# Moving mLSTM's row operations behind the GLA scores in a hybrid decoder step

## The chip, the cores and the metric
The kernel runs on one core of one Trainium2 chip. Its time is the device time of one execution in microseconds, the median of several runs. Five engines work beside each other, each from a queue of its own that it takes in order: TensorE (PE; PEld is its weight load), VectorE (DVE), ScalarE (ACT), GpSimd (POOL) and SyncE (SP, which here only issues transfers).

## The reference
One step of a decoder trunk with two layers, for 512 prompt tokens and 8 sequences of 4 sample tokens, 544 columns in all. Layer 0 ("ab") mixes tokens with two groups of heads, mLSTM and GLA (gated linear attention), layer 1 with a Mamba-2 mixer; each is followed by an MLP. The change is in layer 0's mixer:

```python
mq, mk, mv, mo, mi, mf, gq, gk, gv, gg, ga = split(x @ w_in)      # one projection
# mLSTM, 4 heads of 64 x 128
ig = mi + ig_bias;  lf = log_sigmoid(mf + fg_bias)
b = cumsum(lf);  D = b[t] - b[s] + ig[s]  (s <= t);  m = max(b + m0, max_s D)
s = (q @ k.T) * exp(D - m);  h = (s @ v + ...) / max(|den|, exp(-m))
C = exp(...) * C0 + sum_s exp(D[last, s] - m[last]) * k[s] v[s]
# GLA, 4 heads of 64 x 128
la = log_sigmoid(ga @ wa2 + ba) / 16;  A = cumsum(la)             # per key channel
s[t, s] = sum_k q[t, k] k[s, k] exp(A[t, k] - A[s, k])  (s <= t)
o = s @ v + (q * exp(A)) @ S0
```

## The kernel before
**Dense work.** Activations lie feature-major: 128 features on the partitions, 544 tokens in two halves of 272 (`hf` 0 and 1). A dense product in full precision is three matmuls per 128-deep step: each operand is split into a high part (`whi`, `xh`) and a remainder (`wlo`, `xl`). The projection of layer 0 has 24 weight tiles; each takes 2 halves x 24 matmuls. A tile is loaded by SP (`wraw`), cast by ScalarE (`whi`, L167), and its remainder is taken by VectorE (`wlo`, L168); five tiles are kept ready. The products leave PSUM by ScalarE (L817, L828).

**Lanes.** Everything else in the layer is written as generators, the lanes, which run between the dense matmuls. Before each dense matmul `tick()` moves every lane by one; a lane that yields W["x"] continues W["x"] + 1 matmuls later, and `need(key)` holds it until another lane has marked the key ready. So the order of TensorE's work is counted in dense matmuls by the table `W`. The other engines' order is made by the framework's planner from its own cost model: the earliest ready instruction first, in the order of the program; `tc.high_priority()` moves instructions ahead, and `hold("head")` (L1129, `tc.issue_after`) queues what stands in it behind the last head's last instruction on the same engine.

**The gates.** `gate_sums` (L837) forms the gate columns of the projection for each half, and `gate_rows` (L848) spreads them to rows by one matmul (L852) and copies them with bias into `gate` (L853). When both halves are there, the GLA lane and the mLSTM lane start.

**The GLA lane.** `gla_decay` (L1028) multiplies the gate by wa2 (`la`, L1036), takes the logarithm of the sigmoid and a scan along the tokens (`A`, L1042). `gla_scores` (L1046) works through two halves of the heads, q = 0 and 1. For each it forms the diagonal products (`gd`, L1073), then nine levels of block sizes 1, 2, 4 to 256. For a level GpSimd subtracts (`F`, L1084), ScalarE takes two exponentials (L1086, L1087), VectorE makes the two operands (`zq` L1091, `zk` L1093), and W["lev"] matmuls later TensorE multiplies them (`gs`, L1101, for the last level L1114); the result goes into the score tile `sT` (L1105 and others). W["s0"] is the distance from the start to the first diagonal products. At the end of each half the key ("gT", q) is marked, and behind the second "gscores".

**The heads.** `head_out` (L857) multiplies scores and values (`num`, L868), takes statistics on VectorE (`bst`, `bmv`, `hb`) and normalises on ScalarE (`hf` L878, `hn` L896); 49 matmuls later the result is transposed (`hot`, L902). GLA's heads 0 and 1 follow ("gT", 0), heads 2 and 3 follow ("gT", 1); a head's emission marks ("g", h).

**The mLSTM lane.** `ml_gates` (L1216) works on rows: four partitions (one for each head) of 544 tokens, in the tiles `rw` and `uw`. Block one takes the logarithm of the sigmoid (L1225 to L1228), the scan b (L1229), u = ig - b (L1230) and a running maximum by a second scan (L1236). Block two forms m (L1240), stores it (p_m L1241, s_m L1244), and forms exp(-m) (L1246) and the state weights (L1249 to L1253). Block three (L1257 to L1271) prepares the transposes and the sample tokens. W["gates"] + 1 matmuls after head 3, `uw` is transposed (`uwt`, L1279) to columns for the mLSTM heads, which run after GLA's. In block one the lane waits for ("g", 0), in block two for ("g", 1), in block three for ("g", 2).

## Time and profile before

| | |
|---|---|
| median of 3 runs | 1496.58 us (1495.94 to 1497.34) |
| profiled execution | 1497.35 us, its span 1495.6 us |
| mean granted TensorE clock | 0.994 |
| TensorE busy | 1465.4 us, 98% of the span |
| VectorE, ScalarE, GpSimd busy | 1100.7, 793.6, 190.4 us |
| TensorE's waits in the first 130 us | level products for zk 9.0 us in 2 waits, the longest 7.4; the first matmul 1.1; xh 0.6; la 0.6; gates 0.3 |

Layer 0's mixer fills about the first 260 us. A row of the timeline reads: start, duration, engine, line, operation, what it writes and reads, number of instructions, and in brackets how long the engine stood idle before it and what released it. In a row of waits stand the total, the number and the longest. A row of stretches has the stretch, its length, then for each engine its busy time with the number of instructions, and at the end the granted TensorE clock, the share of the transfer engines and GB/s.

### The profile page before, as it was taken

To read this page: it belongs to the slowest core of one execution; us is meant where nothing else is said; L and a number is where in the kernel's file an instruction comes from. 1 tells how busy PE (TensorE), PEld (TensorE's weight loads), DVE (VectorE), ACT (ScalarE), POOL (GpSimd) and SP (SyncE) were. 2 spreads that over 40 slices of the span, in tenths; PEclk is the share of its full clock that TensorE was granted. 3 is DMA by queue.
4 is the path that set the end of the run, shared out by engine and by line. 5 is a ranking of instruction groups with operands and counts; after the bars stand their busy time and mean duration, and the time that the engine had idled before them with its cause. 6 is when DMAs were issued, how large, how long until landed. Compare 5 with 4: busy or idle time off the path is not lost.

```text
span 1495.6 us, 29198 instructions
## 1 busy us (share of the span) xinstructions
PE 1465.4 (98%) x11607; PEld 1416.8 (95%) x11607; DVE 1100.7 (74%) x2075; ACT 793.6 (53%) x1750; POOL 190.4 (13%) x228
## 2 busy tenths in 40 slices
PE   9989999999999999999999999999999999999997
PEld 8979999999999999999888789899999999999996
DVE  6675676787677667678899978777688677676656
ACT  7455366483444544547786676555257354444343
POOL 2320132100000000010233341421010000000000
PEclk9989999999999999999999999999999999999998
DMA  7202333313233322425557766364222233233121
GB/s 241 81 32 75 100 117 106 104 50 103 87 101 95 100 86 85 156 67 188 130 172 230 246 179 227 99 214 143 71 76 71 96 100 99 85 100 98 59 86 60
DMA packets 95025, 172.51 MB, mean 115 GB/s; under 512 B 15880, under 2 KB 50968, under 8 KB 94632
## 3 DMA queue, kind: packets, MB, share of 16 engines
q1 hardware_dynamic: 62280, 140.44, 29.9%
q10 hardware_dynamic: 29216, 17.19, 4.4%
q0 software_dynamic: 3392, 13.00, 2.4%
q8 instruction: 91, 1.49, 0.4%
q14 instruction: 46, 0.38, 0.1%
HBM read 153.48 MB, written 17.13 MB: 114 GB/s over the span
## 4 chain that ended last, share of the span: by engine, by line
PE 42%; DVE 5%; DMA 2%; issue 1%; ACT 1%; POOL 0%; ACTq 0%; SPq 0%; DVEq 0%; POOLq 0%
PE psd L378 29%; PE psd L590 9%; DMA E<-d_cs 1%; PE yp L1710 1%; PE it L1757 1%; DVE wlo L168 1%; DVE acc L1604 1%; DMA ec<-d_ecs 1%; PE sp L1688 1%; PE sps L1764 1%; DVE h0n L1770 0%; PE ip L1685 0%; ACT E L1670 0%; DVE xf L552 0%; PE xt L1649 0%
## 5 line engine op out<-in xcount | busy, mean ns | idle before, releaser
L378 PE MATMUL psd<-xh,whi 128*128 128x272 f32 x1488 | 440.5, 296 | 0.6 <-ACT xh L287 0.6
L378 PE MATMUL psd<-xl,whi 128*128 128x272 f32 x1488 | 433.8, 292 | 1.3 <-DVE xl L478 1.3
L378 PE MATMUL psd<-xh,wlo 128*128 128x272 f32 x1488 | 434.5, 292 | 0.0
L378 PEld LDWEIGHTS psd<-xh,whi 128*128 128x128 f32 x1488 | 280.5, 189 | 8.4 <-issue 5.1
L378 PEld LDWEIGHTS psd<-xl,whi 128*128 128x128 f32 x1488 | 280.8, 189 | 7.7 <-issue 4.2
L378 PE MATMUL psd<-hh,whi 128*128 128x272 f32 x992 | 286.6, 289 | 0.0
L378 PE MATMUL psd<-hlo,whi 128*128 128x272 f32 x992 | 286.1, 288 | 0.0
L378 PE MATMUL psd<-hh,wlo 128*128 128x272 f32 x992 | 286.0, 288 | 0.0
L378 PEld LDWEIGHTS psd<-xh,wlo 128*128 128x128 f32 x1488 | 280.6, 189 | 4.1 <-issue 3.2
L168 DVE TENSOR_TENSOR wlo<-wraw,whi 128x1024 fp32r<-128x1024 f32 (+2 forms) x175 | 207.3, 1187 | 58.4 <-ACT whi L167 57.4
L167 ACT CAST whi<-wraw 128x1024 fp32r<-128x1024 f32 (+2 forms) x175 | 173.5, 997 | 129.8 <-PE psd L378 115.2
L378 PEld LDWEIGHTS psd<-hh,whi 128*128 128x128 f32 x992 | 186.8, 188 | 0.2
L378 PEld LDWEIGHTS psd<-hlo,whi 128*128 128x128 f32 x992 | 186.7, 188 | 0.2
L378 PEld LDWEIGHTS psd<-hh,wlo 128*128 128x128 f32 x992 | 186.7, 188 | 0.1
L428 DVE TENSOR_TENSOR xf<-xf,psd 128x272 f32<-128x272 f32 x208 | 88.2, 434 | 74.2 <-PE psd L378 73.6
L590 PE MATMUL psd<-xh,wlo 128*128 128x272 f32 x416 | 119.9, 288 | 0.0
L590 PE MATMUL psd<-xh,whi 128*128 128x272 f32 x416 | 119.8, 288 | 0.0
L590 PE MATMUL psd<-xl,whi 128*128 128x272 f32 x416 | 119.6, 288 | 0.0
L203 ACT CAST whi<-wsum 128x1024 fp32r<-128x1024 f32 x52 | 54.3, 1044 | 110.8 <-PE psd L590 70.1
L203 ACT CAST whi<-wraw 128x1024 fp32r<-128x1024 f32 (+1 forms) x52 | 43.4, 834 | 95.3 <-PE psd L378 84.2
L204 DVE TENSOR_TENSOR wlo<-wsum,whi 128x1024 fp32r<-128x1024 f32 x52 | 63.7, 1225 | 23.2 <-ACT whi L203 23.2
L590 PEld LDWEIGHTS psd<-xl,whi 128*128 128x128 f32 x416 | 78.4, 188 | 0.0
(488 smaller groups left out, 2829.7 us busy)
## 6 DMA issues: line engine op xcount, KB each, us to landing
wraw<-mlp_w SPq DMA_DIRECT2D x80, 512.0 KB, 3.6
wraw<-ssd_in SPq DMA_DIRECT2D x40, 512.0 KB, 4.3
wraw<-mlp_w SPq DMA_DIRECT2D x64, 256.0 KB, 2.9
wraw<-ab_in SPq DMA_DIRECT2D x22, 512.0 KB, 3.8
h<-h SPq DMA_DIRECT2D x32, 256.0 KB, 4.2
h0n<-h0n SPq DMA_DIRECT2D x16, 512.0 KB, 4.3
E<-d_cs ACTq DMA_DIRECT2D x16, 512.0 KB, 5.2
s_h<-h0n POOLq DMA_DIRECT2D x16, 512.0 KB, 4.5
```

The source lines that it names most:

```text
L167: nc.scalar.copy(hi[:, r], w[:, r])
L168: nc.vector.tensor_tensor(lo[:, r], w[:, r], hi[:, r].bitcast(F32), ALU.subtract)
L203: self.cut[0] = nc.scalar.copy(hi, x).ins
L204: self.cut[1] = nc.vector.tensor_tensor(lo, x, hi.bitcast(F32), ALU.subtract).ins
L378: last[0] = TE.matmul(ps[:, :TH], (hi, hi, lo)[t][:, k, :], (rh, rl, rh)[t], start=i == 0, stop=i == n - 1).ins
L428: V.tensor_tensor(x, x, ps, ALU.add)
L590: last[0] = TE.matmul(ps, wt[:, k], bt[:, k], start=first and n == 0, stop=n == 11, skip_group_check=not first).ins
L1604: V.scalar_tensor_tensor(acc[:, :n], ci[:, w:w + n], cw[:, m, w:w + 1], acc[:, :n], ALU.mult, ALU.add)
L1688: TE.matmul(sp, Bt[:, b], xw, start=True, stop=True)
L1710: TE.matmul(ypv[64 * e:64 * e + 64, j], z[:, 64 * r:64 * r + 64], E[:, r], start=True, stop=True)
L1757: TE.matmul(it[64 + NS * k:64 + NS * k + NS], Cm[:, NS * (q + k):NS * (q + k) + NS], h0[k], start=q == 0, stop=q == NB - 2)
L1764: TE.matmul(sp[:, 256 * j:256 * j + 256], Xs[:, m * P:(m + 1) * P], Bm.rearrange("p k n -> p (k n)"), start=True, stop=True)
```

## The change
The gates' first half is spread between the first tile's and the second tile's second half, the second half in the middle of the third tile; before, both came behind the second tile. Their two copies get high priority. Block one of the row operations waits for "gscores" and block two for ("g", 2), so that all three blocks are issued behind head 2. W["s0"] goes from 50 to 42, W["lev"] from 15 to 16.

```diff
-W = dict(... lev=15, ... s0=50, ...)
+W = dict(... lev=16, ... s0=42, ...)
@@ gate_rows
-            S.activation(gate[:, c0:c1], p[:, :TH], AF.Identity, bias=gbias)
+            with tc.high_priority():
+                S.activation(gate[:, c0:c1], p[:, :TH], AF.Identity, bias=gbias)
@@ ml_gates
             S.copy(u, gate[0:4])
-            yield from need(("g", 0))
+            yield from need("gscores")
             with hold("head"):
...
-            yield from need(("g", 1))
+            yield from need(("g", 2))
             with hold("head"):
                 m = b
@@ the layer's loop
                 if (hf, m) == (1, 0):
                     for _ in gate_sums(1):
                         pass
-        for hf in range(2):
-            gate_rows(hf)
+                    gate_rows(0)
         for m, key in enumerate(order[:-4]):
             if m >= HEADA:
                 w = ws.next()
                 for hf in range(2):
                     dense(w, xrhs, KT, hf, lambda h, p, m=m: evac(m, h, p))
+                    if (m, hf) == (HEADA, 0):
+                        gate_rows(1)
```

## The prediction
> **What bounds the kernel now.** I read the first part of the page, then the strip of 40 slices, then TensorE's waits, and last the timeline around the one wait that is large.

> ```profile
> span 1495.6 us, 29198 instructions
> PE 1465.4 (98%) x11607; PEld 1416.8 (95%) x11607; DVE 1100.7 (74%) x2075; ACT 793.6 (53%) x1750; POOL 190.4 (13%) x228
> PE gs L1101 <- DVE zk L1093: 9.0, 2, 7.4
> PE la L1036 <- ACT gate L853: 0.6, 1, 0.6
> PE gates L852 <- ACT gsum L846: 0.3, 1, 0.3
> ```

> TensorE is busy 98% of the span, so a change that removes no matmul can only win back idle time or lost clock: 1495.6 - 1465.4 = 30 us are idle in all. In the rows of TensorE's waits, the part that this change touches has three: level products (gs) waiting for VectorE's zk, twice, and two short ones at the gates. The timeline has both level waits and what stands around them.

> ```profile
> 23.05 0.73 PE L852 MATMUL gates<-gsum,selg 128*128 128x272 f32 x2 [0.28 <-ACT gsum L846]
> 25.96 1.19 PE L1036 MATMUL la<-gate,wa 128*128 128x272 f32 x4 [0.56 <-ACT gate L853]
> 41.33 1.05 PE L1101 MATMUL gs<-zq,zk 128*128 128x128 f32 x8
> 48.41 0.41 DVE L1093 TENSOR_TENSOR zk<-gk,F 128x256 f32<-128x256 f32 x1
> 48.88 1.16 PE L1101 MATMUL gs<-zq,zk 128*128 128x128 f32 x8 [1.60 <-DVE zk L1093]
> 91.14 0.29 PE L378 MATMUL psd<-xl,whi 128*128 128x272 f32 x1
> 98.79 2.05 PE L1101 MATMUL gs<-zq,zk 128*128 128x128 f32 x8 [7.36 <-DVE zk L1093]
> 91.43:98.79 7.36, 0.00 (x0) 0.03 (x1) 5.72 (x18) 5.52 (x15) 0.00 (x0) 0.71 0.00 0
> 94.50:95.00 0.50, 0.00 (x0) 0.00 (x0) 0.50 (x1) 0.50 (x2) 0.00 (x0) 0.59 0.00 0
> 98.79:105.46 6.67, 6.67 (x34) 6.67 (x34) 4.50 (x6) 4.62 (x16) 3.45 (x3) 0.55 0.00 0
> ```

> The last three rows are stretches: length, then PE, PEld, DVE, ACT and POOL busy, then the granted TensorE clock. TensorE stands idle from 91.43 to 98.79. The clock falls to half while it waits (0.59 in the half microsecond from 94.50, so some 3.1 us after the idle time began), and stays at a mean of 0.55 over the 6.67 us after the restart. Those 6.67 us hold (1 - 0.55) x 6.67 = 3.0 us of work lost to the clock. The wait of 1.60 us left no mark on the clock. Why zk was late stands in the queues of VectorE and ScalarE:

> ```profile
> 76.68 0.66 ACT L1225 ACTIVATE rw<-rw 4x544 f32<-4x544 f32 x1
> 82.61 0.71 DVE L1228 SCALAR_TENSOR_TENSOR rw<-rw 4x544 f32<-4x544 f32 x1
> 83.36 5.12 POOL L1084 TENSOR_TENSOR F<-A 128x512 f32<-128x512 f32 x3
> 83.53 2.01 DVE L168 TENSOR_TENSOR wlo<-wraw,whi 128x1024 fp32r<-128x1024 f32 x1 [0.20 <-DVE rw L1228]
> 85.57 2.05 DVE L1229 TENSOR_TENSOR_SCAN rw<-con,rw 4x544 f32<-4x544 f32 x1
> 89.52 0.71 DVE L1230 TENSOR_TENSOR uw<-uw,rw 4x544 f32<-4x544 f32 x1
> 90.27 0.43 DVE L1235 TENSOR_SCALAR rw<-con 4x544 f32<-4x544 f32 x1
> 91.14 0.41 DVE L1232 COPY rw<-uw 4x544 f32<-4x544 f32 x1
> 92.35 0.30 ACT L878 ACTIVATE hf<-bmv,epsc 128x4 f32<-128x4 f32 x1 [9.33 <-DVE bmv L873]
> 92.35 1.28 DVE L1236 TENSOR_TENSOR_SCAN rw<-rw 4x544 f32<-4x544 f32 x1
> 94.45 0.72 DVE L1240 TENSOR_TENSOR rw<-rw 4x544 f32<-4x544 f32 x1
> 95.20 0.48 DVE L1249 TENSOR_SCALAR uw<-uw,rw 4x512 f32<-4x512 f32 x1
> 97.11 0.66 ACT L1253 ACTIVATE uw<-uw 4x544 f32<-4x544 f32 x1
> 98.22 0.43 DVE L1093 TENSOR_TENSOR zk<-gk,F 128x256 f32<-128x256 f32 x1 [0.41 <-ACT F L1087]
> ```

> Between 82.61 and 98.65 VectorE runs mLSTM's row operations (four partitions, yet 0.7 us each and 1.28 or 2.05 us for a scan) amid head 1's statistics and the level work. ScalarE waits 9.33 us for those statistics, with the exponentials of the next level queued behind.

> **The change part by part.** No operation is added or removed; places and delays change.

> *Row operations.* The first block (three activations, seven VectorE instructions) waited for head 0, the second (with the two small stores p_m and s_m) for head 1. Both now follow head 2, which comes when the GLA scores are done, where the third block was already. On VectorE that takes 0.71 + 2.05 + 0.71 + 0.43 + 0.41 + 0.13 + 1.28 + 0.72 + 0.48 + 0.18 + 0.16 = 7.3 us out of the 16.0 us from 82.61 to 98.65 (L1233, L1251 and L1243 are the ones under 0.2), and 1.3 us of ScalarE's last two activations stand ahead of the level's exponentials besides. Without them zk is ready at about 98.65 - 7.3 = 91.4 at the latest. When does TensorE want it? Delays are counted in dense matmuls, 0.125 us each. The gates' second half comes 24 matmuls later, the first products 8 sooner, each level one later: by the fourth level of the second half of the heads 24 - 8 + 9 + 4 = +29, or 3.6 us, less 2.4 us of earlier waits that go (below). So it is wanted at about 92.5, 1.1 us after zk is ready. Gain: 7.36, and the 3.0 of the clock. Ends: all 10.4, or nothing if zk stays as late (a rival).

> [...]

> *The third level of the first half* (the 1.60 us). TensorE would come to it 24 - 8 + 3 = 19 matmuls or 2.4 us later, less the 0.84 below: at 47.28 + 1.5 = 48.8, and its zk was done at about 48.8. Gain 1.6 if VectorE keeps its order; ends 0 (all of it shifts along) and 1.6. The cover of the first level is thicker too: its zk must be there at 41.33 + 17 matmuls - 0.84 = 42.6.

> *The two urgent copies and the gates' places.* The first half's matmul moves 24 matmuls ahead and the second behind the third tile's first half, so that only one copy is left in the 12 matmuls (1.5 us) between the second and la, and it goes ahead of waiting weight casts. Gain 0.56 + 0.28 = 0.84; ends 0 and 0.84, since a weight cast of 1.05 us that has just begun still goes first.

> *What it costs.* The row operations end in the transposes uwt, which need all of them:

> ```profile
> 120.17 2.40 PE L868 MATMUL num<-vt,sT 128*128 128x128 f32 x20
> 123.91 0.16 DVE L893 SCALAR_TENSOR_TENSOR hb<-bmv,hf 128x4 f32<-128x4 f32 x1 [0.60 <-ACT hf L879]
> 124.11 0.44 DVE L1257 TENSOR_SCALAR uw<-rw 4x544 f32<-4x544 f32 x1
> 126.28 0.81 ACT L896 ACTIVATE hn<-num,hb,hf 128x128 f32<-128x128 f32 x2
> 131.95 0.48 DVE L872 BATCH_NORM_STATS2 bst<-num 128x6 f32<-128x128 f32 x2
> 134.58 1.23 DVE L168 TENSOR_TENSOR wlo<-wraw,whi 128x1024 fp32r<-128x1024 f32 x1 [1.12 <-ACT whi L167]
> 136.87 0.60 PE L1279 MATMUL uwt<-con,uw 128*128 128x128 f32 x4
> 124.10:136.90 12.80, 12.80 (x108) 12.80 (x107) 9.71 (x33) 7.13 (x20) 0.84 (x1) 1.00 0.16 45
> ```

> The distance from head 2's products (120.17) to uwt (136.87) is set by unchanged delays: 16.7 us. Head 2's last hn ends at 127.1, and 1.4 us earlier if a weight cast and a copy do not stand between, as here. From there: three activations of 0.66 (2.0), then on VectorE 0.71 + 1.28 + 0.71 + 0.41 + 0.13 + 0.43 + 1.28 + 0.72 + 0.44 + 0.48 + 0.18 = 6.8 (a scan at its undisturbed 1.28), then one activation of 0.66: 9.5 us in a row. In between VectorE owes head 3's statistics (about 1.6: two rows as the one shown, and as many small ones) and one weight remainder (1.23): 12.3. From 125.7 to 127.1 this ends at 138.0 to 139.4, so uwt would come 1.1 to 2.5 us late; what else VectorE does there (it is busy 9.71 of 12.80 us) adds something. I take 2.4, the upper part. Ends: 0, since the planner may see the lateness and let dense matmuls go ahead of uwt, and from the row where the same chain ran before: 97.77 - 76.68 = 21.1 us, which from 127.1 would be 11.3 late, with 3.0 for the clock. Behind the row operations on ScalarE stand weight casts and copies out of PSUM, for which five weight tiles and the free banks are cover; p_m and s_m stand in SP's queue ahead of weight loads, which they would hold for as long as the rows are late, less than the same cover of several tiles at 6 us each. Without that cover, another wait of the same length.

> What follows is late next only by 34 matmuls (4.3 us): the mLSTM heads start that much later and there is dense work left to cover them.

> **Sum.** 7.36 + 3.0 + 1.6 + 0.84 - 2.4 = 10.4 us. The profiled execution took 1497.35 against a median of 1496.58, so its own time would be 1486.95 and the median 1486.2.

> **Rivals.** First, uwt does not wait at all (the planner's order, or the chain at its shortest): 12.8 us gained, 1483.8. For it: everything else in these queues is placed by the planner where it thinks it ready. Against: it had the level's products at 91.4 too, and zk came at 98.65.

> Second, uwt waits beyond the point where the clock falls, some 3.1 us: a wait of 3.5 with 3.0 for the clock costs 6.5, gain 6.3, 1490.3. For it: 2.4 is near, and VectorE has little room. [...] The price here is from the rows above.

> Third, the wait at the fourth level of the second half stays, because head 1 and GpSimd's F hold it (three F take 5.12 us from 83.36, and a weight remainder beside them 2.01 instead of 1.23), and not the rows: then only the 2.4 us of small waits go and uwt takes them back, 1496.6. Against: 7.3 of 16.0 us are the rows' own.

> Fourth, slower: the row chain at its new place takes longer than at the old. At 21.1 us it costs 11.3 + 3.0 = 14.3 against 12.8, 1498.1; it decides against the change at 19.6 us, and at 25 us the time is 1502.0. For it: the third block, the sample scores and head 3 share VectorE. Against: GpSimd, which slowed the scan from 1.28 to 2.05, is busy 0.84 of 12.8 us there.

> **How the numbers follow.** Chances: forecast 0.52 (1484.5 to 1488.5, the small terms and uwt between their ends), no wait 0.18, wait with clock 0.18, no change 0.06, longer than before 0.06. About 0.2% (3 us) is what a measurement can tell here. Faster 0.88, same 0.07, slower 0.05. The range takes in the first two rivals: 1482.5 to 1491.5.

> **What would show it.** In the profile after: no wait of gs for zk at the second half's fourth level and a granted clock of 1.00 from 80 to 120 us; the waits at la and gates gone; L1225 and L1228 behind the last level's products; uwt 87 matmuls after head 2's products, with a wait for VectorE or ScalarE of 0 to 3 us. It would be wrong if uwt or the mLSTM heads wait more than 5 us, or a level product waits again.

## The result, and the profile after

The change makes the kernel slower by half a per cent: 1505.38 us (median of 7 runs, 1499.49 to 1508.47) against 1496.57 (7 runs, 1495.94 to 1497.64). The ratio is 1.0051, with a 95% interval of 1.0034 to 1.0068. The forecast was 1486.2, so the sign was wrong. The profiled execution took 1502.27 us at a mean granted clock of 0.993; the median run had 0.991, the slowest 0.988. The runs of this kernel differ by 9 us, those of before by 1.7.

The page after, and then TensorE's waits in the first 300 us (engine, line and tile <- what released it: total, number, longest):

```profile
span 1500.6 us, 29204 instructions
PE 1468.2 (98%) x11607; PEld 1419.1 (95%) x11607; DVE 1100.2 (73%) x2075; ACT 795.0 (53%) x1750; POOL 192.8 (13%) x228
```

```profile
PE uwt L1280 <- ACT uw L1254: 3.0, 1, 3.0
PE gs L1102 <- DVE zk L1094: 2.7, 2, 2.0
PE supd L1008 <- POOL vm L1004: 2.3, 2, 2.0
PE mkt L1367 <- ACT hn L897: 1.5, 1, 1.5
PE rowbc L769 <- DVE E L1322: 1.4, 1, 1.4
...
PE sc L1288 <- DVE rw L1271: 0.9, 1, 0.9
```

From the gates' copies on, line numbers are one or two higher than in before. The wait of 7.4 us is down to 2.0, and la and gates no longer wait. In exchange there are new kinds of wait. The five longest are at uwt (the transposed rows), sc (the sample tokens' columns, made from the rows), rowbc (which spreads a row over the partitions for an mLSTM head), mkt (transposed sample keys) and supd (the update of the sample states, for which GpSimd forms vm). The timeline puts them in order:

```profile
48.01 1.05 PE L1102 MATMUL gs<-zq,zk 128*128 128x128 f32 x8
95.17 1.13 PE L1102 MATMUL gs<-zq,zk 128*128 128x128 f32 x8 [1.96 <-DVE zk L1094]
114.29 2.40 PE L869 MATMUL num<-vt,sT 128*128 128x128 f32 x20
134.21 0.87 PE L1280 MATMUL uwt<-con,uw 128*128 128x128 f32 x4 [3.04 <-ACT uw L1254]
138.58 1.01 PE L1288 MATMUL sc<-ones,rw 4*128 4x2 f32 x4 [0.94 <-DVE rw L1271]
189.94 0.51 PE L769 MATMUL rowbc<-rb,selr 128*128 128x256 f32 x2 [1.36 <-DVE E L1322]
196.68 0.33 PE L1367 MATMUL mkt<-con,gkz 128*128 128x128 f32 x1 [1.55 <-ACT hn L897]
221.81 0.92 PE L1008 MATMUL supd<-vm,gkstk 128*128 128x390 f32 x2 [2.04 <-POOL vm L1004]
280.06 0.62 PE L458 MATMUL mu<-lns,ones 128*128 128x272 f32 x2
```

The same first matmul behind the mixer (mu, the sums for a layer norm) in before:

```profile
274.44 0.62 PE L458 MATMUL mu<-lns,ones 128*128 128x272 f32 x2
```

Three marks give the balance. Head 2's products stood at 120.17 in before. Now they start at 114.29, and in the program they come 34 dense matmuls (4.3 us) later than they did. So 5.9 + 4.3 = 10.1 us were won up to there. At mu the kernel is 280.06 - 274.44 = 5.6 us behind. From mu to the end of the span both take nearly the same (1221.2 us in before, 1220.5 in after). So 15.7 us are lost between head 2 and the end of the mixer. The waits there add up to 3.04 + 0.94 + 0.25 (a first supd) + 1.36 + 1.55 + 2.04 = 9.2. The rest is the clock, in two stretches (length, then PE, PEld, DVE, ACT, POOL busy, granted clock, share of the transfer engines, GB/s):

```profile
134.20:144.50 10.30, 9.35 (x41) 8.62 (x41) 4.87 (x18) 4.73 (x12) 0.00 (x0) 0.51 0.15 53
223.30:226.60 3.30, 3.30 (x15) 3.11 (x14) 1.53 (x6) 0.97 (x3) 0.76 (x1) 0.50 0.85 351
```

They cost 0.49 x 9.35 = 4.6 and 0.50 x 3.30 = 1.7 us. 9.2 + 4.6 + 1.7 = 15.5 of the 15.7.

**Why uwt is late.** The row chain at its new place, first and last instructions and those that stood between (start, duration):

```profile
119.93 0.66 ACT L1226 ACTIVATE rw<-rw 4x544 f32<-4x544 f32 x1
120.61 1.05 ACT L167 CAST whi<-wraw 128x1024 fp32r<-128x1024 f32 x1
121.98 0.66 ACT L1227 ACTIVATE rw<-rw 4x544 f32<-4x544 f32 x1
...
123.37 0.72 DVE L1229 SCALAR_TENSOR_TENSOR rw<-rw 4x544 f32<-4x544 f32 x1
127.88 0.75 DVE L905 TENSOR_SCALAR cg<-hot,prm 128x512 f32<-128x512 f32 x1
132.15 1.11 DVE L1250 TENSOR_SCALAR uw<-uw,rw 4x512 f32<-4x512 f32 x1
133.50 0.66 ACT L1254 ACTIVATE uw<-uw 4x544 f32<-4x544 f32 x1 [0.70 <-DVE uw L1252]
```

It starts 5.6 us after head 2's products (the working had 5.5 to 6.9) and takes 134.16 - 119.93 = 14.2 us instead of 12.3. What the working did not have in it: a weight cast and a copy on ScalarE between the first two activations (1.4 us), the operation for cg on VectorE (0.75) and an operation that took 1.11 us instead of 0.48 (0.63). The weight remainder that it had counted (1.23) ran beside ScalarE's activations instead. That makes 1.5 of the 1.9 us.

**Where 2.0 us stay at the level.** Its exponentials (L1087) still come behind head 1's hf and hn on ScalarE, which had waited 5.47 us for statistics:

```profile
89.36 0.30 ACT L879 ACTIVATE hf<-bmv,epsc 128x4 f32<-128x4 f32 x1 [5.47 <-DVE bmv L874]
92.15 1.50 ACT L897 ACTIVATE hn<-num,hb,hf 128x128 f32<-128x128 f32 x4 [0.82 <-DVE hb L894]
93.54 0.42 ACT L1087 ACTIVATE F<-F 128x256 f32<-128x256 f32 x1
```

Between hf and hn stand a weight cast on ScalarE (1.05 us) and its remainder on VectorE (1.23 us), so hn starts 2.8 us after hf. In e1 below neither stands there, hn starts 0.8 us after hf, and the level waits 0.88. Every run with moved rows and the later lanes (after, e3, e4, e7, e10) has the 1.96 us, every one with moved rows and without them (e1, e5, e6, e8) 0.88 or 0.89. That this queue is the cause was not tested by itself.

**Why supd waits.** On GpSimd four transfer issues for the next stage (xf) now stand directly ahead of vm. In after:

```profile
218.69 2.20 POOL L325 DMA_DIRECT2D xf<-xT  x4
220.90 1.42 POOL L1004 TENSOR_TENSOR vm<-vstk,con 128x390 f32<-128x390 f32 x2
```

In before they came two by two, the second pair behind a wait, and vm was done without a wait of TensorE:

```profile
206.71 1.15 POOL L325 DMA_DIRECT2D xf<-xT  x2
209.90 1.07 POOL L325 DMA_DIRECT2D xf<-xT  x2 [2.05 <-PE num L868]
```

### The profile page after: what moved, and what is told of

Read it like the earlier page. It is cut to its first block, busy times and chain, and to the rows that moved or that the text cites. A ratio compares the mean times of both kernels' runs of the same rounds, so it can differ in the third digit from the quotient of the medians.

```text
span 1500.6 us, 29204 instructions
## 1 busy us (share of the span) xinstructions
PE 1468.2 (98%) x11607; PEld 1419.1 (95%) x11607; DVE 1100.2 (73%) x2075; ACT 795.0 (53%) x1750; POOL 192.8 (13%) x228
## 4 chain that ended last, share of the span: by engine, by line
PE 44%; DVE 5%; DMA 1%; issue 1%; ACT 1%; SPq 0%; DVEq 0%
PE psd L378 30%; PE psd L590 9%; PE yp L1712 1%; DVE wlo L168 1%; DVE acc L1606 1%; PE it L1759 1%; PE sp L1690 1%; PE ip L1687 1%; PE sps L1766 1%; DMA wraw<-mlp_w 0%; DVE h0n L1772 0%; PE xt L1651 0%; DMA ec<-d_ecs 0%; DVE xf L552 0%; DVE Y L1715 0%
## 5 line engine op out<-in xcount | busy, mean ns | idle before, releaser
L378 PE MATMUL psd<-xh,whi 128*128 128x272 f32 x1488 | 441.3, 297 | 1.0 <-ACT xh L287 1.0
L378 PE MATMUL psd<-xl,whi 128*128 128x272 f32 x1488 | 435.5, 293 | 1.3 <-DVE xl L478 1.3
L378 PE MATMUL psd<-xh,wlo 128*128 128x272 f32 x1488 | 435.7, 293 | 0.0
L378 PEld LDWEIGHTS psd<-xl,whi 128*128 128x128 f32 x1488 | 281.8, 190 | 7.9 <-issue 4.0
L378 PEld LDWEIGHTS psd<-xh,whi 128*128 128x128 f32 x1488 | 281.4, 189 | 8.0 <-issue 4.7
L378 PE MATMUL psd<-hh,whi 128*128 128x272 f32 x992 | 286.9, 289 | 0.0
L378 PE MATMUL psd<-hlo,whi 128*128 128x272 f32 x992 | 286.5, 289 | 0.0
L378 PE MATMUL psd<-hh,wlo 128*128 128x272 f32 x992 | 286.4, 289 | 0.0
L378 PEld LDWEIGHTS psd<-xh,wlo 128*128 128x128 f32 x1488 | 281.6, 189 | 4.4 <-issue 3.5
L168 DVE TENSOR_TENSOR wlo<-wraw,whi 128x1024 fp32r<-128x1024 f32 (+2 forms) x175 | 206.6, 1184 | 54.3 <-ACT whi L167 52.8
L167 ACT CAST whi<-wraw 128x1024 fp32r<-128x1024 f32 (+2 forms) x175 | 173.5, 997 | 130.2 <-PE psd L378 108.6
L378 PEld LDWEIGHTS psd<-hlo,whi 128*128 128x128 f32 x992 | 186.9, 188 | 0.2
L378 PEld LDWEIGHTS psd<-hh,whi 128*128 128x128 f32 x992 | 186.9, 188 | 0.2
L378 PEld LDWEIGHTS psd<-hh,wlo 128*128 128x128 f32 x992 | 186.9, 188 | 0.1
```

The costliest lines, as they stand in the source:

```text
L167: nc.scalar.copy(hi[:, r], w[:, r])
L168: nc.vector.tensor_tensor(lo[:, r], w[:, r], hi[:, r].bitcast(F32), ALU.subtract)
L378: last[0] = TE.matmul(ps[:, :TH], (hi, hi, lo)[t][:, k, :], (rh, rl, rh)[t], start=i == 0, stop=i == n - 1).ins
```

## The experiments

Three theories were open. Late rows: their new place makes uwt late enough to lose the clock, and this is all that is lost. Lost cover: what stands behind the GLA scores starts 34 matmuls later (24 by the gates, -8 by s0, 18 by the levels), and all of it, the mLSTM heads and the state updates, meets other work in the queues and loses its cover. Other cause: the level's wait did not come from the rows at all. "Shift" below means those 34 matmuls. W["lev"] = 15 with W["s0"] = 26 undoes them with the gates at their new places. Before ran on the same chip beside each group, at 1495.97 (the first four), 1495.51 (e5, e6, e7, e8) and 1495.75 (e9, e10, e11).

### e1: the rows alone

Before, with the two waits of the row blocks as in the change:

```diff
-            yield from need(("g", 0))
+            yield from need("gscores")
...
-            yield from need(("g", 1))
+            yield from need(("g", 2))
```

> Kernel before with the two waits of the row operations moved alone (gates, copies and both delays as before, so no lane is shifted). Theory A (the change loses twice: about 8.5 us where uwt waits for the row chain, with the clock, and about 7 us in waits among the mLSTM heads, because every lane behind the scores comes 34 matmuls later, against the gg and mo tiles): the wait of 7.4 us at the fourth level goes to under 3 us, uwt waits 2 to 4 us with the clock falling, the 1.6 us wait stays, and there are no new waits among the mLSTM heads: 1494 to 1499 us. Theory B (the row operations at their new place make the later waits too, by the order that the planner then chooses): the later waits of 1.4, 1.6 and 2.0 us come here as well, 1501 to 1505 us.

1496.87 us, ratio 1.0004 (0.9995 to 1.0014). TensorE's wait at uwt, and the clock behind it:

```profile
PE uwt L1279 <- ACT uw L1253: 5.2, 1, 5.2
```

```profile
131.57:145.60 14.03, 14.03 (x60) 13.36 (x61) 5.68 (x19) 3.11 (x8) 1.88 (x2) 0.50 0.01 2
```

The level's wait falls from 7.4 to 0.9, so the rows were its cause. But uwt waits 5.23 us and then 14.0 us of work run at half clock, which is 7.0 us. The gain is spent. The row chain starts 6.9 us after head 2's products here, behind a weight cast and a copy, and takes 15.1 us (5.6 and 14.2 in after), which is why uwt is later than there. Among the mLSTM heads nothing waits beyond 0.2 us.

### e2: everything but the rows

After, with the two waits back at ("g", 0) and ("g", 1), so shift, gates and copies stay.

> The changed kernel with the row operations back behind heads 0 and 1; gates, urgent copies and the two delays as changed. Theory A: no wait at uwt, the waits at the gates and the third level gone, the fourth level of the second half waits 5 to 7 us with the clock, and the waits among the mLSTM heads (3 to 5 us, perhaps a fall of the clock) are there, since the lanes are shifted: 1497 to 1502 us. Theory B: no waits among the mLSTM heads: 1491 to 1495 us.

1500.59 us, ratio 1.0025 (1.0015 to 1.0034). Waits of TensorE:

```profile
PE gs L1102 <- DVE zk L1094: 9.3, 2, 8.3
PE supd L1008 <- POOL vm L1004: 2.3, 2, 2.1
```

The 7.4-us wait has not moved away with the shift; it is 8.32. uwt does not wait, but supd does, as in after. So the shift by itself costs time, and late rows alone do not explain the loss. (e11 below is this kernel without the shift, and 5.2 us faster.)

### e3: uwt later

After, with W["gates"] from 30 to 54, so that uwt comes 24 dense matmuls (3.0 us) later.

> The changed kernel with W['gates'] 54 instead of 30: uwt is 24 matmuls (3.0 us) later. Theory A: the wait at uwt falls under 0.5 us and that at the sample columns with it, the clock stays full there, so some 8 us come back; the mLSTM heads start 17 matmuls later and keep their waits or gain some: 1496 to 1501 us. Rival: whoever waits is only moved (cols and the row broadcast are late instead): 1503 to 1507 us.

1497.85 us, ratio 1.0010 (1.0001 to 1.0018), 7.5 below after.

```profile
PE supd L1008 <- POOL vm L1004: 3.3, 2, 3.0
PE hot L903 <- ACT hn L897: 2.8, 1, 2.8
```

uwt and sc no longer wait, and most of what they cost comes back. Part of the wait has moved: head 3's transposes (hot) now wait 2.77 us for hn, whose scale hb stands behind the rows and a weight remainder on VectorE, and supd waits 3.00.

### e4: block one in a stretch where VectorE is idle

VectorE in before has a gap of 7.17 us behind the last level of the first half:

```profile
70.82 1.23 DVE L168 TENSOR_TENSOR wlo<-wraw,whi 128x1024 fp32r<-128x1024 f32 x1 [7.17 <-ACT whi L167]
```

After, with block one right behind that level's operands; blocks two and three stay behind head 2:

```diff
                     gla["last"] = [x.ins for x in f]
+                    if (q, L) == (0, 256):
+                        ready.add("levels0")
...
-            yield from need("gscores")
-            with hold("head"):
+            yield from need("levels0")
+            with hold():
```

> The changed kernel with block one of the row operations right behind the last level's operands of the first half of the heads, where VectorE stood idle for 7.2 us (62.97 to 70.82 in the kernel before); blocks two and three stay behind head 2. Theory A: 5.7 us of VectorE's 7.3 leave the stretch before uwt, which waits under 0.5 us with a full clock, and the fourth level's wait of the second half stays at 2 us or less; the waits among the mLSTM heads stay: 1495 to 1499 us. Theory B: those go too: 1487 to 1491 us. Against both: head 0's statistics come late behind the scan, and the levels of the second half with them: 1502 us or more.

1491.28 us, ratio 0.9969 (0.9957 to 0.9980), 14.1 below after.

```profile
PE gs L1104 <- DVE zk L1094: 2.7, 2, 2.0
PE supd L1008 <- POOL vm L1004: 2.3, 2, 2.1
```

```profile
96.00:100.00 4.00, 4.00 (x23) 4.00 (x22) 2.50 (x4) 2.00 (x6) 2.24 (x3) 0.57 0.01 4
212.00:216.00 4.00, 4.00 (x19) 3.55 (x17) 1.79 (x6) 1.83 (x5) 0.96 (x2) 0.57 0.99 407
```

The waits at uwt and sc are gone and with them the long clock fall; so late rows are one part of the loss. The level's 1.96 us stay, so here it is not the rows that hold zk. Two clock falls remain, each behind a wait of only 2.0 or 2.1 us.

### e5 and e6: the same without the shift

e5 is before with e4's edit and block two behind ("g", 2), gates and copies as before. e6 is e4 with W["lev"] = 15 and W["s0"] = 26.

> Kernel before with the row operations alone moved: block one behind the last level of the first half of the heads, blocks two and three behind head 2; gates, copies and delays as before, so no lane is shifted. Theory A (idle VectorE takes the rows free of cost, the later waits come from the shift of the lanes by 34 matmuls): the fourth level waits under 2 us, uwt not at all, the 1.6 us at the third level and 0.8 us at the gates stay, no waits among the mLSTM heads: 1496 - 6 to 10 = 1486 to 1490 us. Rival (the gates' early start is needed for the gain): 1491 to 1495 us.

> The kernel with block one in the hole and the changed gates (1491.3 us), with W['lev'] 15 and W['s0'] 26, so that everything behind the scores comes 0 matmuls later than in the kernel before instead of 34. Theory A: the waits at supd (2.1 and 0.2 us) and the fall of the clock there (1.7 us) go; against that the levels are wanted 1 matmul sooner each and the first one 16 sooner, so the level waits may grow by up to 2 us in the first half: 1486 to 1492 us. Rival (the waits at supd are the planner's, not the shift's): they stay, 1490 to 1495 us.

e5: 1487.80 us, ratio 0.9947 (0.9933 to 0.9960). e6: 1486.50 us, ratio 0.9945 (0.9932 to 0.9957). Both beat the kernel before and after. Block one on VectorE in e6 (the first, the two scans), and its largest wait:

```profile
61.92 0.71 DVE L1231 SCALAR_TENSOR_TENSOR rw<-rw 4x544 f32<-4x544 f32 x1
63.46 1.28 DVE L1232 TENSOR_TENSOR_SCAN rw<-con,rw 4x544 f32<-4x544 f32 x1
66.64 1.28 DVE L1239 TENSOR_TENSOR_SCAN rw<-rw 4x544 f32<-4x544 f32 x1
```

```profile
PE gs L1104 <- DVE zk L1094: 2.9, 3, 1.6
```

```profile
20.00:280.00 260.00, 256.91 (x2078) 247.76 (x2077) 184.08 (x452) 144.46 (x334) 60.85 (x67) 1.00 0.31 98
```

No supd wait, and a granted clock of 1.00 from 20 to 280 us (last row). e5 has the gates at their old places and gains as much (mu at 263.40), so the gain is that of the rows in the gap. e4 and e6 differ by the shift alone: it costs 4.8 us even where uwt does not wait (at mu, in the traces, 269.92 against 264.06).

### e7: the exponentials first

e4 with `tc.high_priority()` around the two exponentials of a level.

> The kernel with block one in the hole (1491.3 us), with high priority for the two exponentials of each level. Theory: the wait of 2.0 us left at the fourth level comes from ScalarE's queue, where the exponentials stand behind head 1's hf and hn, which wait for VectorE; in front of them they let zk come in time, so the wait of 2.0 and its clock fall (some 1.7 us) go: 1487 to 1490 us. Rival (zk is late for VectorE's own queue or for GpSimd's F): 1490 to 1493 us, the wait as before.

1491.01 us, ratio 0.9971 (0.9962 to 0.9980), and the wait is still 1.96 us. The planner left the exponentials behind head 1's hf and hn (93.91 us, with F ready since 86.6), so the edit did not change the queue and tells nothing of the cause.

### e8: the change without the shift

After, with W["lev"] = 15 and W["s0"] = 26.

> The changed kernel (1505.4 us) with W['lev'] 15 and W['s0'] 26 alone: rows still behind head 2, everything behind the scores 0 matmuls later than in the kernel before instead of 34. Theory A: uwt still waits 3 to 5 us with the clock (8 to 14 us in all), but the waits among the mLSTM heads (1.4, 1.6, 2.0 us and a clock fall of 1.7) go: 1496 to 1500 us. Rival (those waits follow from the late row chain, not from the shift): they stay, 1503 to 1506 us.

1496.03 us, ratio 1.0002 (0.9992 to 1.0011): 9.4 below after.

```profile
PE uwt L1280 <- ACT uw L1254: 5.2, 1, 5.2
```

As in e1, uwt alone spends the gain, with 14.2 us of work at half clock, and the mLSTM heads have their cover. What separates this from after is the shift.

### e9: a part of the shift

e6 with W["s0"] = 38, a shift of 12.

> The kernel with block one in the hole, the changed gates and no shift (1486.5 us), with W['s0'] 38 instead of 26: the first products are wanted 12 matmuls later, and so is everything behind. Theory A: the waits of 1.6 us at the first and 0.4 us at the third level go, a shift of 12 brings at most half a microsecond at supd: 1484 to 1486 us. Rival (a shift of 12 is enough for the xf transfers to fall ahead of vm): a wait of 2 us at supd again, 1486 to 1490 us.

1488.34 us, ratio 0.9954 (0.9941 to 0.9966), not below e6. The waits at the levels fall from 2.9 to 1.4 us, supd does not wait, and a new wait comes among the mLSTM heads:

```profile
PE hot L903 <- ACT hn L897: 1.1, 1, 1.1
```

In the traces the mixer itself is 0.65 us shorter than in e6 (mu at 263.41 against 264.06). The clock falls twice in layer 1 (at 720 and 833 us, 1.7 us of work each), where e6's trace has no fall; a total time that is not lower therefore does not show that the 12 matmuls cost time in the mixer.

### e10: the transfers of the next stage off GpSimd's queue

e4 with the four xf loads issued by SP.

> The kernel with block one in the hole and the lanes shifted by 34 (1491.3 us), with the four loads of xf issued by SP instead of GpSimd. Theory: with the shift these four issues (2.2 us) stand in GpSimd's queue right ahead of a vm that supd waits for; without them the wait of 2.1 us at supd and its fall of the clock go, the waits at the fourth level (2.0) and the first (0.7) stay: 1486.5 to 1489 us. Rival (vm is late for VectorE's or ScalarE's sake): wait and time as before, 1490 to 1493 us; or SP's queue holds weight loads back behind the four: a wait for whi or wlo.

1488.83 us, ratio 0.9957 (0.9944 to 0.9969), 2.5 below e4; the two intervals overlap a little, but in the traces mu comes 3.7 us earlier (266.25 against 269.92).

```profile
PE supd L1008 <- POOL vm L1004: 0.2, 1, 0.2
```

```profile
206.00:216.00 10.00, 10.00 (x75) 9.31 (x74) 7.86 (x35) 5.86 (x15) 2.96 (x4) 1.00 0.92 326
```

The wait of 2.08 us is gone (0.24 of another stay), and the clock stays at 1.00 through that stretch: supd waited for GpSimd's queue, where the issues stood ahead of vm.

### e11: the gates and copies alone

After, without shift and with the rows at their old places.

> The gates' places and the urgent copies alone: row operations behind heads 0 and 1 as in the kernel before, W['lev'] 15 and W['s0'] 26, so that nothing behind the scores is shifted. Theory A: the waits at gates and la (0.8 us) go, the first level waits 1 to 1.6, the third 0.4, the fourth of the second half still 6 to 8 with the clock; no wait at uwt, none among the mLSTM heads: 1494 to 1497 us. Rival (the early gates alone relieve the fourth level): 1486 to 1491 us.

1495.43 us, ratio 0.9998 (0.9989 to 1.0007): no difference.

```profile
97.54 2.04 PE L1102 MATMUL gs<-zq,zk 128*128 128x128 f32 x8 [7.35 <-DVE zk L1094]
```

la and gates no longer wait, and the first level waits 1.31 us instead.

## Why the prediction was wrong, step by step

**Right: the cause of the large wait.** Rows out of the way, 7.36 us become 1.96 (0.9 in e1), while with the rows in place they stay (8.32 in e2, 7.35 in e11). The third level's 1.60 and the 0.84 at la and gates went as worked out; its products stand at 48.01, for which 48.8 was given. Up to head 2 the steps promised 12.8 us and 10.1 came: 1.96, 0.73 and 0.30 of small waits are left. "zk is ready at about 98.65 - 7.3 = 91.4 at the latest" was too early: in after the exponentials that it needs stand behind head 1 on ScalarE until 93.54.

**Wrong: "What it costs", put at 2.4 us.** It was 3.04 for uwt, 0.94 for sc and 4.6 for the clock, 8.6 in all. The second rival had the mechanism (a fall beyond some 3.1 us) at a wait of 3.5 and 3.0 for the clock; here 3.04 was enough, and the half clock lasted 10 us, with sc's wait in it. The 3.1 us, read from one wait of before, were no threshold: the 2.04 us at supd lost the clock as well (last section). The second fall lasted 3.41 us, the first 10.24, and those of e1 and e8 17.1, of which 14.2 were work without a wait. That a wait of this length has a price with a step in it should have moved the chances: 2.4 with a working uncertain by 2 us is as likely to fall as not.

The lower end, "the planner may see the lateness and let dense matmuls go ahead of uwt", was no possibility. In this layer TensorE's order is that of the program (`tc.manual_schedule` for that engine); the planner orders the others only.

**Wrong: "there is dense work left to cover them", put at zero.** Behind the scores 0.25 + 1.36 + 1.55 + 2.04 = 5.2 us went to waits and 1.7 to the clock. The supd waits are the shift's: e2 and e4 have them (2.1 us the longest), e6 and e8 do not. The fall of the clock stands behind them in after (223.26) and e4 (212.22). The wait at rowbc and most of that at mkt need the shift and the late rows together: e2 and e4, with the shift and block one early, have 0 and 0.34, and e1 and e8, with late rows and no shift, have neither. This step had named its cover without looking whether it reached 34 matmuls further, and had not looked at GpSimd's queue, where the next stage's transfers follow whatever comes late. From 8.6 - 2.4 = 6.2, 6.9 here and 2.7 at head 2, less the 0.6 that came back behind mu, follow the 15.2 us between forecast and profiled execution (1486.95 and 1502.27: 15.3). The fourth rival had the sign, but not the mechanism: the chain took 14.2 us, not 19.6.

That leaves 3.1 us between this profiled execution and the median of 1505.38. The median run had the lower mean clock (0.991 against 0.993, which over 1500 us is 3.0), and nothing else is on record for it.

**What stays open.** The 1.36 us at rowbc are read, not tested. In after, VectorE's queue has the last update of a sample state behind a gg operation that waits 2.25 us for ScalarE. So the store of that state is issued 3.0 us after its supd ends (0.7 in e4, where the update stands ahead of gg), VectorE then stands 2.44 us until the store has freed the buffer, and rowbc waits for the next operation behind that, E. Why mkt waits 1.55 us was not followed. What brings the clock back is open: in e1 it stayed at half through 14.0 us of work without a wait, in after's second fall through 3.3. A version with both the row blocks in the gap and xf on SP without the shift was not tried.

## What to carry to other kernels

Work that delays an engine's queue is better put where that engine is idle, as block one in the gap of 7.17 us, than behind the next thing it feeds. The wait otherwise turns up there. A lane that is started later uses up slack at its end: look at the last consumers and at every queue they pass, the transfer issues on GpSimd among them, before putting the delay at zero. Of the waits of about 2 us here some were followed by a fall of the clock (2.04 us in after, 1.96 and 2.08 in e4) and one was not (1.96 in after), so give such a wait both prices.

## What the runs showed of the hardware

In after a wait of 2.04 us was enough to lose the clock, and it was lost after work had resumed. TensorE stands idle from 219.77 to 221.81 before supd, and the half clock begins at 223.26, 3.5 us after the idle time began; in before it was 3.2 us (91.43 to 94.59).

```profile
93.55:96.96 3.41, 1.79 (x15) 1.82 (x16) 2.97 (x5) 2.33 (x9) 1.37 (x2) 1.00 0.35 138
219.84:223.26 3.42, 1.45 (x8) 1.18 (x9) 2.05 (x6) 1.89 (x7) 2.47 (x4) 1.00 0.90 317
92.75:96.16 3.41, 1.45 (x13) 1.41 (x13) 2.55 (x4) 2.35 (x8) 1.37 (x1) 1.00 0.49 144
136.25:139.66 3.41, 1.68 (x9) 1.11 (x10) 3.09 (x11) 3.10 (x9) 0.23 (x1) 1.00 0.46 131
```

TensorE is idle for 3.41 - 1.79 = 1.62 us in the first, and no fall follows. In the others it is idle for 1.97, 1.96 and 1.73 us, and each ends with a fall. In before a step with 1.60 us of idle time (46.80 to 50.21) goes without a fall, and the one with 3.16 (91.17 to 94.59) ends with one. (Further on, two steps of layer 1 with 1.84 and 1.87 us, in e4 and e7, went without one, so 1.73 us is no fixed bound.) Of the level's wait of 1.96 us in after, 0.34 lay in the step before (93.21 to 93.55), and no fall followed; in e4 all of it lay in one step (92.82 to 94.78), and the half clock behind it cost 1.7 us of work. By single waits, behind the first 10 us and up to 300 us in the traces of after, before, e1 and e3 to e11: those up to 1.61 us (e1) went without a fall, the 1.96 us went without one in after and had one behind them in e3, e4, e7 and e10, and each wait from 2.04 us on had one.

The falls go with the spread of the runs: 9 us in after, at mean clocks of 0.988 to 0.996, against 2.3 in e6, whose profile has no fall in this stage. In after, while GpSimd worked on vm beside it (0.83 us from 132.15), one VectorE operation on four partitions took 1.11 us (L1250) instead of the 0.48 of before (L1249).
